# A two-block model on one core: the memory's value projection in the first stage, with uncut float32 operands

## The chip, the cores and the metric

The kernel runs on one core of a Trainium2 chip. The metric is the device time of one execution in microseconds; a time given for a kernel is the median of several runs. Five engines work in one core: TensorE (PE; its weight loads are listed apart as PEld), VectorE (DVE), ScalarE (ACT), GpSimd (POOL) and SyncE (SP), which here issues most DMA transfers.

## The reference, cut to what matters

The model has two blocks over 256 tokens of width 1024: a first block of two layers (a sliding-window attention beside a state-space mixer, then a stick-breaking attention, each followed by a gated feed-forward), and a second block with a feed-forward, a gated mixer, a cross attention to a memory of 256 tokens, and a last feed-forward. The change touches one projection of the cross attention:

```python
def memory_cross_attention(h, m, wq, wk, wv, wo):
    b, s, _ = h.shape
    nm = m.shape[1]
    q = (h @ wq).reshape(b, s, X_HEADS, X_HEAD_DIM)
    k = (m @ wk).reshape(b, nm, X_HEADS, X_HEAD_DIM)
    v = (m @ wv).reshape(b, nm, X_HEADS, X_HEAD_DIM)
    ...
    return o.reshape(b, s, D_MODEL) @ wo
```

Here `m = rmsnorm_2(mem, mem_norm)`. `m @ wv` (256x1024 by 1024x1024) depends on inputs alone, so it can be computed at any time before the cross attention.

## The kernel before

**Weights.** All weight matrices are packed into slabs of 128 partitions by 2048 float32 (1 MB), in the order of use. A slab is loaded over the SP queue into a tile `raw`, of which there are two buffers (`_make`, L270 to L298). Each half of the slab is then cut in two parts in the reduced format fp32r: ScalarE casts it to `whi` (L293), VectorE subtracts to get the rest `wlo` (L295); there are five buffers of half a slab for each. The `raw` buffer is free when both parts of both halves are made. A slab is asked for two slabs ahead of its use (`W_AHEAD`).

**Operands.** The activations are cut in the same way: `_norm` (L443) multiplies the input by the norm's gain, as a high part on ScalarE (L453) and a low part on VectorE (L454), in tiles `a` (four buffers). It also sums the squares: ScalarE squares (L461), GpSimd adds (L463). The inverse root mean square is made in `inv_rms`: column sums on TensorE (L419), a power on GpSimd (L424). It is applied after the product.

**Products.** A product of two cut operands takes three fp32r matmuls (`mm3`, L314 to L322): high by high, high by low, low by high. With operands of one part, `mm3` issues one matmul instead.

**The first stage** (`even`, up to about 130 us). The order in which its parts are written is the string `EVEN`: `p` are the projections of queries, keys and values, `h` the head norms, `i` the four input steps of the state-space mixer, `t` and `s` its tables and scan, `m` and `g` its output products, two digits a step of the window attention, `x` the building of the state matrices on GpSimd (L927 to L929, into tiles `a`), and `N`, `W0` to `W3` the memory's norm and the four slabs of `m @ wv`, each a 256-column part of `mv` (`memory`, L486). The parts of the state matrices are issued on GpSimd after the head norm's last power (`rqk`, L407 and L408), which needs the sums of squares `ssh` (ScalarE L782, VectorE L783). The products of `W` go to an accumulator tile `acc`, of which there are four in PSUM; the state-space inputs hold two of them until the scan has read them. The kernel is written with a framework that orders the instructions of every engine by priority and by a simulated time, so that the order on the engines is not that of the text. Behind the four `W` slabs the plan has two slabs of the output projection, the mixer's gate, and two more output slabs; the first output matmuls are those of `acc<-et,whi`.

In the second block's mix stage, the memory is normed a second time for the keys (`K0` to `K3`), with operands in a pool of that stage.

Of the kernel before, what the change touches and what calls it, by code (L numbers as in the profile page):

```python
# [12 lines left out]
AF = mybir.ActivationFunctionType  # L13
# [3 lines left out]
P = 128  # L17
# [35 lines left out]
def weight_plan():  # L53
# [29 lines left out]
    for f in EVEN.split():  # L83
        if f == "p0":
            tok("even_w_in", 0, 0)
        elif f == "p1":
            feat("even_w_in", 0, 512, 256)
        memory(f)
# [5 lines left out]
    for f in ODD.split():  # L94
        if f[0] == "v":
            tok("odd_w_in", 0, 2048 + int(f[1]) * 512)
        elif f[0] in "qk":
            feat("odd_w_in", 0, (f[0] == "k") * 1024 + int(f[1]) * 256, 256)
        memory(f)
# [4 lines left out]
    for f in MIX.split():  # L104
        if f[0] in "vwxy":
            tok("w_in", 0, 512 + "vwxy".index(f[0]) * 512)
        elif f[0] == "u":
            feat("w_in", 0, int(f[1]) * 256, 256)
        memory(f)
# [13 lines left out]
PR_GAIN, PR_BGLU, PR_ONA, PR_ONB, PR_QN, PR_KN, PR_ARE, PR_AIM, PR_LDT = (  # L123
    0, 80, 84, 88, 92, 93, 94, 110, 126)
# [113 lines left out]
class Kernel:  # L238
# [29 lines left out]
        return self.t(self.sm, shape, tag, dt, bufs)  # L268


    def _make(self, upto, first=None):
        nc = self.nc
        while self.made <= min(upto, len(self.plan) - 1):
            s = self.made
            raw = self.t(self.wp, [P, 2048], "raw", bufs=2)
            if first is None:
                nc.sync.dma_start(raw, self.a["wts"][s])
            else:

                for h, then in enumerate(first):  # L280
                    c = slice(h * 512, (h + 1) * 512)
                    nc.sync.dma_start(self.xt[:, 2 * h:2 * h + 2, :],
                                      self.a["x"][:, c].rearrange("p (b t) -> p b t", b=2))
                    then()
                    nc.sync.dma_start(raw[:, c], self.a["wts"][s][:, c])
            parts = []
            n = 1024 if first is None else 512
            for h in range(2):
                hi = self.t(self.wp, [P, 1024], "whi", F32R, bufs=self.W_BUFS)
                lo = self.t(self.wp, [P, 1024], "wlo", F32R, bufs=self.W_BUFS)  # L290
                for c in range(0, 1024, n):
                    src = raw[:, h * 1024 + c:h * 1024 + c + n]
                    nc.scalar.copy(hi[:, c:c + n], src)  # L293
                    with self.tc.issue_after(self.pin) if self.pin and s > 1 else nullcontext():
                        nc.vector.tensor_tensor(lo[:, c:c + n], src, hi[:, c:c + n].bitcast(F32), ALU.subtract)  # L295
                parts.append((hi, lo))
            self.split[s] = parts
            self.made += 1  # L298
# [144 lines left out]
    def _norm(self, x, gain, tag, make, pool, soon):  # L443
        nc = self.nc
        ops = None
        if make:
            ops = [self.operand(pool, f"m{i}") for i in range(2)]
        ssq = self.t(self.wk, [P, 512], "ssq")
        for pr in range(4):
            for b in (2 * pr, 2 * pr + 1) if make else ():  # L450
                g = self.prm[:, PR_GAIN + gain * 8 + b:PR_GAIN + gain * 8 + b + 1]
                hi, lo = ops[b // 4][0][:, b % 4, :], ops[b // 4][1][:, b % 4, :]
                nc.scalar.activation(hi, x[:, b, :], AF.Copy, scale=g)  # L453
                lo = nc.vector.scalar_tensor_tensor(lo, x[:, b, :], g, hi.bitcast(F32),  # L454
                                                    ALU.mult, ALU.subtract).ins
            q = ssq if pr == 0 else self.t(self.wk, [P, 512], "sq", bufs=2)
            xf = x[:, 2 * pr:2 * pr + 2, :].rearrange("p b t -> p (b t)")
            if gain == 0 and SQE[pr] != "a":
                (nc.gpsimd if SQE[pr] == "g" else nc.vector).tensor_tensor(q, xf, xf, ALU.mult)
            else:  # L460
                nc.scalar.activation(q, xf, AF.Square)  # L461
            if 0 < pr < 3 or pr == 3 and not soon:
                nc.gpsimd.tensor_tensor(ssq, ssq, q, ALU.add)  # L463
        if soon:
            sqs = []
            for x, e in zip((ssq, q), FOLD[gain]):
                if e != "-":
                    (nc.gpsimd if e == "g" else nc.vector).tensor_tensor(x[:, :256], x[:, :256], x[:, 256:], ALU.add)
                sqs += [x[:, c:c + 256] for c in ((0, 256) if e == "-" else (0,))]
        else:  # L470
            nc.gpsimd.tensor_tensor(ssq[:, :256], ssq[:, :256], ssq[:, 256:], ALU.add)
            sqs = [ssq[:, :256]]
        if x is self.xt and make and self.at:
            pin, self.pin = self.pin, lo if PINN else self.pin
            self._make(self.at - 1 + self.W_AHEAD)
            self.pin = pin
        rb, rs = self.inv_rms(sqs, D, 1e-6, tag)
        return ops, rb, rs
# [7 lines left out]
    def memory(self, f, how, pool=None):  # L486
        nc = self.nc
        c = int(f[1:] or 0)
        if f[0] == "N":
            mem = self.t(self.wp, [P, 2048], "raw", bufs=2).rearrange("p (b t) -> p b t", b=8)  # L490
            self.load_feat(mem, self.a["mem"], nc.sync)
            self.mops, self.mrb, self.mrs = self.norm(mem, 8, "mrb", haste=False, pool=pool, soon=how[1])
        elif f[0] == "K":
            if not self.kt:
                self.kt = self.t(self.late, [P, 8, 256], "kt")
            self.gemm_feat(self.mops, "cross_wk", 0, c * 256, 256,
                           self.scaled(self.kt[:, 2 * c:2 * c + 2, :], self.mrb), how[0])
        else:
            if not self.mv:
                self.mv = [self.t(self.values, [P, D], f"mv{t}") for t in range(NT)]  # L500
            w = self.slab("cross_wv", 0, "f", 0, c * 256)
            ps = self.ps(how[0])
            for half in range(2):
                for t in range(NT):
                    for k in range(4 * half, 4 * half + 4):
                        self.mm3(ps[:, t * 256:(t + 1) * 256], self.lhs(self.mops, k, t), w(k * 256, 256),
                                 k == 0 and t == 0, k == 7)
            for t in range(NT):
                nc.scalar.activation(self.mv[t][:, c * 256:(c + 1) * 256], ps[:, t * 256:(t + 1) * 256],
                                     AF.Copy, scale=self.mrs[t])  # L510
# [1055 lines left out]
```

## Time and profile before

| | |
|---|---|
| median of 3 runs | 1231.01 us (1229.61 to 1231.33) |
| the profiled execution | 1231.68 us |
| its span, first to last instruction | 1230.0 us |
| PE busy | 1195.4 us (97%), 7678 matmul records |
| DVE busy | 861.5 us (70%) |
| ACT busy | 681.6 us (55%) |
| POOL busy | 193.4 us (16%) |
| mean granted TensorE clock | 0.987 |

Busy times are of one execution. A busy PE is not a PE at its peak, since matmuls overlap each other: the time between the starts of two matmuls says more than the duration of one.

### The profile page before, as it was taken

How to read it: one execution, taken by the hardware profiler on the slowest of the kernel's cores; microseconds unless marked ns; L12 is line 12 of the kernel's file. 1: busy time of each engine (PE TensorE's matmuls, PEld its weight loads, DVE VectorE, ACT ScalarE, POOL GpSimd, SP SyncE). 2: the span in 40 equal slices, each digit the busy share in tenths (PEclk: the TensorE clock that was granted, in tenths of full speed). 3: DMA queues.
4: the chain of work that ended last, by engine and by line, in shares of the span. 5: the costliest groups of instructions: out<-in, count | busy, mean ns of one | idle time of the engine just before them, and what ended most of it. 6: DMA issues, size and time to landing. Idle time of an engine off the chain costs nothing.

```text
span 1230.0 us, 19039 instructions
## 1 busy us (share of the span) xinstructions
PE 1195.4 (97%) x7678; PEld 1061.6 (86%) x7678; DVE 861.5 (70%) x1196; ACT 681.6 (55%) x1063; POOL 193.4 (16%) x164
## 2 busy tenths in 40 slices
PE   6889999999999999999999999999999999999997
PEld 6767988888898888888888888888879999888886
DVE  8988588776666548777767776666865666777752
ACT  7544565664456757555545655545554545655542
POOL 2295031110010003111002101003201102111000
PEclk9988999999999999999999999999999999999998
DMA  6632345555553234555655555556623534455660
GB/s 241 200 121 87 123 172 202 178 202 202 175 178 137 103 138 171 174 203 179 219 191 184 191 192 184 183 199 203 215 100 104 175 108 162 174 199 178 206 205 35
DMA packets 36777, 208.86 MB, mean 170 GB/s; under 512 B 3921, under 2 KB 9809, under 8 KB 12753
## 3 DMA queue, kind: packets, MB, share of 16 engines
q1 hardware_dynamic: 35824, 205.48, 48.4%
q0 software_dynamic: 576, 1.64, 0.5%
q8 instruction: 60, 0.98, 0.3%
q10 hardware_dynamic: 288, 0.52, 0.1%
q14 instruction: 29, 0.23, 0.1%
HBM read 205.57 MB, written 2.06 MB: 169 GB/s over the span
## 4 chain that ended last, share of the span: by engine, by line
PE 74%; DMA 8%; DVE 7%; ACT 5%; POOL 3%; issue 3%; SPq 0%; DVEq 0%; ACTq 0%; POOLq 0%
PE acc L367 23%; PE acc L366 12%; PE mm L367 10%; DMA raw<-in_wts 6%; PE mm L366 5%; PE acc L321 3%; PE acc L320 3%; PE acc L322 3%; PE mm L320 3%; PE mm L321 3%; PE mm L322 3%; DVE wlo L295 3%; ACT whi L293 3%; POOL a L927 1%; DMA raw<-in_mem 1%
## 5 line engine op out<-in xcount | busy, mean ns | idle before, releaser
L295 DVE TENSOR_TENSOR wlo<-raw,whi 128x1024 fp32r<-128x1024 f32 (+1 forms) x378 | 470.5, 1248 | 235.1 <-ACT whi L293 233.1
L293 ACT CAST whi<-raw 128x1024 fp32r<-128x1024 f32 (+1 forms) x378 | 393.1, 1046 | 279.5 <-DMA raw<-in_wts 117.1
L367 PE MATMUL mm<-a,whi 128*128 128x512 f32 x704 | 247.0, 392 | 0.0
L367 PE MATMUL acc<-h,whi 128*128 128x512 f32 x704 | 246.8, 396 | 0.0
L367 PE MATMUL acc<-a,whi 128*128 128x512 f32 x704 | 245.8, 391 | 0.0
L366 PE MATMUL acc<-h,wlo 128*128 128x256 f32 x704 | 196.9, 281 | 0.4 <-ACT h L549 0.4
L366 PE MATMUL mm<-a,wlo 128*128 128x256 f32 x704 | 196.5, 281 | 0.0
L366 PE MATMUL acc<-a,wlo 128*128 128x256 f32 x704 | 196.2, 280 | 0.0
L367 PEld LDWEIGHTS acc<-h,whi 128*128 128x128 f32 x704 | 131.8, 188 | 31.0
L367 PEld LDWEIGHTS mm<-a,whi 128*128 128x128 f32 x704 | 131.5, 187 | 28.5
L367 PEld LDWEIGHTS acc<-a,whi 128*128 128x128 f32 x704 | 130.9, 187 | 28.1
L366 PEld LDWEIGHTS acc<-a,wlo 128*128 128x128 f32 x704 | 133.0, 189 | 0.9
L366 PEld LDWEIGHTS acc<-h,wlo 128*128 128x128 f32 x704 | 132.9, 189 | 1.1 <-ACT h L549 0.7
L366 PEld LDWEIGHTS mm<-a,wlo 128*128 128x128 f32 x704 | 132.6, 189 | 0.2
L546 POOL TENSOR_TENSOR sg<-sg,rb 128x512 f32<-128x512 f32 x44 | 58.3, 1326 | 391.7 <-ACT sg L545 391.7
L463 POOL TENSOR_TENSOR ssq<-ssq,sq 128x512 f32<-128x512 f32 x26 | 40.2, 1544 | 420.6 <-ACT sq L461 250.1
L320 PE MATMUL mm<-a,whi 128*128 128x256 f32 x224 | 65.3, 293 | 7.3 <-ACT whi L293 6.4
L321 PE MATMUL acc<-a,whi 128*128 128x256 f32 x240 | 67.6, 285 | 0.0
L322 PE MATMUL acc<-a,wlo 128*128 128x256 f32 x240 | 67.4, 285 | 0.0
L322 PE MATMUL mm<-a,wlo 128*128 128x256 f32 x224 | 64.8, 290 | 1.4 <-DVE wlo L295 1.3
L320 PE MATMUL acc<-a,whi 128*128 128x256 f32 x240 | 65.9, 285 | 0.0
L321 PE MATMUL mm<-a,whi 128*128 128x256 f32 x224 | 64.5, 289 | 0.0
(369 smaller groups left out, 1912.3 us busy)
## 6 DMA issues: line engine op xcount, KB each, us to landing
raw<-in_wts SPq DMA_DIRECT2D x187, 1024.0 KB, 4.9
raw<-in_mem SPq DMA_DIRECT2D x4, 512.0 KB, 5.7
eb<-lag SPq DMA_DIRECT2D x4, 512.0 KB, 5.2
x<-in_x SPq DMA_DIRECT2D x4, 256.0 KB, 5.1
raw<-in_wts SPq DMA_DIRECT2D x4, 256.0 KB, 5.3
sprm<-in_prm SPq DMA_DIRECT2D x1, 512.0 KB, 9.4
ud<-s SPq DMA_DIRECT2D x1, 512.0 KB, 3.2
uu<-ud SPq DMA_DIRECT2D x8, 64.0 KB, 5.9
```

Of the source, the lines that this page charges most:

```text
L293: nc.scalar.copy(hi[:, c:c + n], src)
L295: nc.vector.tensor_tensor(lo[:, c:c + n], src, hi[:, c:c + n].bitcast(F32), ALU.subtract)
L320: mm(out, a[0], b[0], start=start, stop=False, skip_group_check=True)
L321: mm(out, a[0], b[1], start=False, stop=False, skip_group_check=True)
L322: mm(out, a[1], b[0], start=False, stop=stop, skip_group_check=True)
L366: mm(out[:, 0, :], w[1], x[:, 0], start=first, stop=False, skip_group_check=True)
L367: mm(out, w[0], x, start=False, stop=last, skip_group_check=True)
L463: nc.gpsimd.tensor_tensor(ssq, ssq, q, ALU.add)
L546: nc.gpsimd.tensor_tensor(sg, sg, rb2, ALU.mult)
L927: eng.tensor_tensor(out, f(pr), h(xr), ALU.mult)
```

## The change

The four slabs of `cross_wv` are no longer cut: the slab's halves in `raw` are handed to the product as one-part operands of float32. The memory's operand in the first stage is one float32 tile of 8 blocks (memory times gain, on ScalarE), again of one part, so `mm3` issues one float32 matmul where it issued three fp32r ones. The second norm of the memory, in the mix stage, keeps its cut operands.

```diff
+    @staticmethod
+    def whole(key):
+
+        return key[0] == "cross_wv"
+
     def _make(self, upto, first=None):
...
+            if self.whole(self.plan[s]):
+                self.split[s] = [(raw[:, :1024],), (raw[:, 1024:],)]
+                self.made += 1
+                continue
             parts = []
...
     def _norm(self, x, gain, tag, make, pool, soon):
         nc = self.nc
         ops = None
-        if make:
+        if make == "whole":
+            y = self.t(self.ap4, [P, 8, 256], "a", bufs=self.A_BUFS)
+            ops, make = [(y[:, :4],), (y[:, 4:],)], False
+            for b in range(8):
+                g = self.prm[:, PR_GAIN + gain * 8 + b:PR_GAIN + gain * 8 + b + 1]
+                nc.scalar.activation(y[:, b, :], x[:, b, :], AF.Copy, scale=g)
+        elif make:
             ops = [self.operand(pool, f"m{i}") for i in range(2)]
...
-            self.mops, self.mrb, self.mrs = self.norm(mem, 8, "mrb", haste=False, pool=pool, soon=how[1])
+            self.mops, self.mrb, self.mrs = self.norm(mem, 8, "mrb", pool is not None or "whole", haste=False,
+                                                      pool=pool, soon=how[1])
```

## Rows read from the trace of the kernel before

**Rows 1.** Stretches: length, busy time (instructions) of five engines, clock, DMA share, GB/s.
```profile
44.00:62.00 18.00, 15.89 (x149) 14.79 (x147) 16.90 (x24) 11.42 (x24) 7.36 (x6) 0.91 0.52 185
78.00:98.00 20.00, 14.86 (x136) 10.43 (x136) 14.99 (x24) 7.56 (x26) 19.22 (x17) 0.79 0.22 66
105.00:130.00 25.00, 24.55 (x246) 21.71 (x245) 18.95 (x29) 13.48 (x29) 4.36 (x4) 1.00 0.40 130
130.00:1230.00 1100.00, 1086.18 (x6771) 967.83 (x6771) 754.62 (x1023) 609.42 (x914) 130.22 (x107) 1.00 0.49 171
```

**Rows 2.** Instructions of TensorE in order of time: start, duration, line, operation, out<-in, count.
```profile
104.94 0.38 PE L320 MATMUL acc<-whi,a 128*128 128x256 f32 x1
...
110.67 0.28 PE L322 MATMUL acc<-whi,a 128*128 128x256 f32 x1
...
118.63 0.28 PE L322 MATMUL acc<-whi,a 128*128 128x256 f32 x1
...
119.33 0.32 PE L1088 MATMUL acc<-a,sprm 128*64 128x128 f32 x1
...
129.29 0.60 PE L320 MATMUL acc<-et,whi 128*128 128x256 f32 x3
```

**Rows 3.** GpSimd in order of time; in brackets idle time before and its releaser.
```profile
59.40 1.09 POOL L424 TENSOR_TENSOR rs<-rs,nhalf 128x2 f32<-128x2 f32 x1 [6.10 <-DVE rs L423]
61.61 0.78 POOL L407 TENSOR_SCALAR rqk<-ssh 128x10 f32<-128x10 f32 x1 [1.11 <-DVE ssh L783]
...
70.91 2.09 POOL L927 TENSOR_TENSOR a<-sp_pr,sp_nci 128x512 f32<-128x512 f32 x1
...
76.07 2.08 POOL L927 TENSOR_TENSOR a<-sp_pr,sprm 128x512 f32<-128x512 f32 x1
...
79.17 1.09 POOL L927 TENSOR_TENSOR a<-sp_pr,sprm 128x512 f32<-128x512 f32 x1
...
93.78 1.26 POOL L929 TENSOR_TENSOR eb<-eb,otmpg 128x512 f32<-128x512 f32 x1
```

**Rows 4.** VectorE in order of time.
```profile
60.10 1.23 DVE L295 TENSOR_TENSOR wlo<-raw,whi 128x1024 fp32r<-128x1024 f32 x1 [0.17 <-ACT whi L293]
61.24 0.28 DVE L783 TENSOR_REDUCE ssh<-sq 128x2 f32<-128x128 f32 x1
...
69.90 4.18 DVE L295 TENSOR_TENSOR wlo<-raw,whi 128x1024 fp32r<-128x1024 f32 x2
...
101.19 0.68 DVE L1037 TENSOR_TENSOR s<-acc,s2c 128x512 f32<-128x512 f32 x1
...
114.81 1.35 DVE L1051 TENSOR_TENSOR bdc<-eb,s 64x496 f32<-64x496 f32 x2
```

**Rows 5.** ScalarE in order of time.
```profile
53.09 0.47 ACT L769 ACTIVATE qkv<-mm,rs 128x256 f32<-128x256 f32 x1
59.01 1.06 ACT L293 CAST whi<-raw 128x1024 fp32r<-128x1024 f32 x1 [5.44 <-DMA raw<-in_wts]
59.97 0.83 ACT L782 ACTIVATE sq<-qkv 128x128 f32<-128x128 f32 x2
```

**Rows 6.** Cross scores on TensorE: durations (min/median/max ns) of line L1415; part in order of time.
```profile
L1415 PE MATMUL mm<-kt,qt x32: 377/379/382, 987.5 to 1004.9; 128*128 128x256 f32 x32
...
988.46 2.75 PE L1415 MATMUL mm<-kt,qt 128*128 128x256 f32 x12
```

**Rows 7.** Groups of VectorE, 25 to 130 us: count | busy us, mean ns | idle before.
```profile
L295 DVE TENSOR_TENSOR wlo<-raw,whi 128x1024 fp32r<-128x1024 f32 x18 | 24.1, 1350 | 2.8 <-ACT whi L293 2.8
```

**Rows 8.** Loads issued by SP, in order of time.
```profile
39.98 0.85 SPq L658 DMA_DIRECT2D raw<-in_mem  x2
43.31 15.10 SPq L277 DMA_DIRECT2D raw<-in_wts  x3
...
66.44 8.00 SPq L277 DMA_DIRECT2D raw<-in_wts  x2
```

**Rows 9.** DMA issues of the page: count, KB each, us to landing.
```profile
raw<-in_wts SPq DMA_DIRECT2D x187, 1024.0 KB, 4.9
```

## The prediction

> **What bounds the kernel now.** I read the stretches first, then the chain of waits, then each engine's instructions in order of time along it. From 130 us to the end TensorE's matmuls are busy 1086.2 of 1100 us [rows 1]: nothing of the change lies there, and a time won or lost before 130 us is handed on whole. Before it TensorE has holes: 14.9 of 20 us from 78 to 98, at a granted clock of 0.79 [rows 1]. From 105 on it is full again, 24.55 of 25 us [rows 1]. So the question is what sets the moment at which the first output projection starts, 129.29 us [rows 2].
>
> The chain of waits, read backwards from there, leads through TensorE to GpSimd's `eb` of the last state step, which ends at 95.04, and GpSimd comes there through an almost unbroken run of outer products that starts behind the head norm's two `rqk` pairs; the first starts at 61.61, released by VectorE's reduction `ssh` [rows 3]. That reduction (61.24) stands behind a `wlo` at 60.10 [rows 4], and its squares (59.97) stand on ScalarE behind the cast `whi` at 59.01, which had idled 5.44 us for a weight load [rows 5]. By order of the loads that slab is W2, the third of the four touched here. VectorE is busy 16.9 of 18 us from 44 to 62 [rows 1]. So a slab that nobody needs until the cross stage holds up the head norm, and with it GpSimd.
>
> **The change, part by part.** All sums stand against the profiled execution, 1231.68 us (a span of 1230.0 and 1.7 around it); the median shown, 1231.01, is 0.7 lower.
>
> *TensorE.* Removed: 4 slabs x 16 products x 3 reduced matmuls = 192. W2's 48 start between 104.94 and 110.67, so 5.73/47 = 0.122 us each [rows 2]: 5.85 a slab. Added: 64 uncut matmuls of 128x256. The cross scores are this very form: 16 matmuls in the program, 32 records, 12 of them in 2.75 us, the last lasting 0.38, so 2.37/11 = 0.215 us a record [rows 6], two records a matmul, 0.43 us. 16 x 0.43 = 6.9 us a slab, +1.05; over four slabs +4.2. W0 and W1 run earlier, while the chain is on VectorE and GpSimd: cost 0, and +2.1 if that cover is gone. W2 and W3 run in the full stretch after 104.94: **+2.1**. At the lower of the clock's levels all of these double; the stretch after 105 was granted 1.00 [rows 1].
>
> The rule that speaks against the change agrees in kind and differs in size. The Trainium skill (FP8 and Floating Point Precision, TensorE Precision Notes) says that true float32 takes four passes through the array. With the reduced matmul's step for a pass that is 4 x 0.122 = 0.49 us a product, +2.0 a slab, so +4.0 instead of +2.1 here; the two records of the row are shorter than that, and I go by the row.
>
> *VectorE and ScalarE.* Eight `wlo` halves go, 1.35 us each on average [rows 7], eight `whi` halves of 1.06 [rows 5], and the memory's eight `a` subtractions. The eight scaled copies on ScalarE stay in number, as uncut ones. The part on the path: W2's cast no longer stands before the squares. At least its wait of 5.44 goes; at most all from the end of the second `qkv` copy (53.09 + 0.47 = 53.56) to the end of that cast (60.07), 6.5 us [rows 5]. At the other end 0, or worse, is the second rival below. I take **-5.4**, the wait itself: the memory's own work on ScalarE now comes later (next part) and will eat some of the rest.
>
> *GpSimd.* Its outer-product multiply takes 2.09 us at 70.91, while VectorE works on W3's two `wlo` (69.90 to 74.08, 2.09 each instead of a typical 1.2), and 1.09 us at 79.17 without one [rows 3, 4]. Three such long ones start between 70.91 and 76.07 (2.09, 2.09, 2.08); the first two lie beside W3's. Those `wlo` go: 2 x 1.0 = **-2.0**, on the chain. Bounds: 0, if other two-input work of VectorE moves in beside them; -3.0, if the third goes too (its `wlo` is the first output slab's, which is only moved).
>
> *The raw buffers.* There are two, and an uncut slab holds its own until its matmuls have read it. W0 thus holds one while the memory wants one: the memory's load, at 39.98 before, now waits for the next projection slab's split, after which the following weight load went at 43.31 [rows 8], so +3.3 us on the memory. W1's load waits for the memory as before; W2's and W3's for W0's and W1's matmuls; and the first two output slabs, loaded at 66.44 and 74.11 [rows 8], now for W2's and W3's. The last of W3's matmuls ends about 119 [rows 2]. A load lands after 4.9 us [rows 9]; two casts and a subtraction make the second output slab ready some 8.2 us after W3's end. It is wanted one slab (5.8 us) after the first output matmul, and that follows W3's end by 10: wanted after 16, there after 8. Cost 0; were the 8 us of cover gone, each microsecond more would cost one. The same moves bring one more split into the stretch from 105 to 130, where VectorE has 6 us free: 0, at most 1.2.
>
> *The operand.* One tile instead of two, in the same slots: nothing waits for a slot there, 0.
>
> Sum: -5.4 - 2.0 + 2.1 = -5.3, so 1226.4 for an execution like the profiled one and **1225.7** against the median. With 0 to -6.5, 0 to -3.0 and +2.1 its own range is 1222 to 1229.
>
> **Rivals.**
>
> *W2 goes into the hole.* Uncut, W2 is ready when its load lands. If it is put behind W1 before 98 us, the stretch after 105 loses a slab. Then VectorE's scan limits it: the last state copy ends at 116.16 [rows 4], the state products start at 119.33 [rows 2]: -3.2, and the +2.1 is hidden. Total -5.4 - 2.0 - 3.2 = -10.6: 1220.4. For: TensorE's hole. Against: W2's product needs one of four accumulator banks, and started soon after the scan's readings of the two state banks (101.19 to 101.87) [rows 2, 4].
>
> *Slower: the memory norm stays ahead on GpSimd.* The memory's power (59.40) stands before the `rqk` pairs in GpSimd's queue [rows 3]. If it keeps that place while the memory's load is 3.3 us later, it ends at about 63.8 and `rqk` starts there or later: +2.2 on the chain at the least, +3.3 if all behind it slides. With +2.1 to +4.2 from TensorE and the -2.0 given back by later collisions, that is +4.3 to +7.5. I take +4.3: 1235.3. It decides as soon as the memory's power stands before the first `rqk`. For: it did before. Against: the squares of the heads are then ready some 5 us before it, and the queue's order follows readiness.
>
> *A wash.* The head norm comes forward by only the 2.1 that W2 and W3 cost, because the memory's twelve copies and squares on ScalarE push in front of the head norm's, and the collisions on GpSimd only change partners: 1231.
>
> *It doesn't do what it says.* Were an uncut product run as one reduced pass, four slabs would cost a third of 23.4 us, but the scores' two records a product [rows 6] speak against it.
>
> **How the numbers follow.** Forecast 0.42; W2 in the hole 0.20; slower 0.20; wash 0.12; an order laid out anew for other reasons 0.06, half of it slower. What this measurement can tell from no change is 0.2%, 2.5 us. Faster: 0.42 x 0.95 + 0.20 + 0.02 = 0.62; within: 0.12 + 0.02 + 0.01 = 0.15; slower: 0.23. The range goes from W2 in the hole with all bounds on its side, 1217, to the slower case, 1236; about 0.2 stays outside.
>
> **What would show it.** Right: `rqk` starts at 55 to 57; no idle of 5 us on ScalarE before the head squares; the outer products about 1.1 us throughout 62 to 75; `eb` ends near 87.6; a W slab's 32 records take 6.9 us; the first output matmul stands at about 124. Wrong: the first `rqk` at or after 61; W2's records before 98 (first rival); ScalarE idling for the second output slab's load, or TensorE idling before it; any change after 130 us that is not a mere shift.

## The result, and the profile after

The changed kernel takes **1253.41 us** (median of 4 runs, 1249.46 to 1258.57), the kernel before 1231.17 (4 runs): a ratio of 1.0169 [1.0147, 1.019]. It is slower by 22 us; I had said 1225.7. Its profiled execution took 1254.56 us, a span of 1252.8. Lines up to the products stand 9 further down in its text, those of the first stage 16.

The same stretches as in [rows 1], of the changed kernel; columns as there:

```profile
44.00:62.00 18.00, 18.00 (x144) 16.20 (x141) 8.87 (x14) 9.48 (x22) 10.55 (x9) 1.00 0.49 165
78.00:98.00 20.00, 19.32 (x109) 12.94 (x108) 10.63 (x20) 6.78 (x22) 11.56 (x9) 0.50 0.07 19
105.00:130.00 25.00, 23.20 (x115) 18.47 (x112) 16.49 (x22) 6.34 (x18) 9.70 (x7) 0.79 0.27 87
130.00:1230.00 1100.00, 1087.76 (x6818) 967.54 (x6817) 759.38 (x1027) 614.02 (x923) 127.83 (x105) 1.00 0.50 173
```

VectorE is relieved from 44 to 62 (8.87 us busy, 16.9 before), as meant. From 78 to 98 TensorE is busy almost throughout, at a granted clock of 0.50, its lower level, and from 105 to 130 the clock is 0.79 where it was 1.00.

GpSimd, against [rows 3]:

```profile
54.48 0.21 POOL L416 TENSOR_SCALAR rqk<-ssh 128x10 f32<-128x10 f32 x1 [2.13 <-DVE ssh L799]
...
57.75 0.69 POOL L433 TENSOR_TENSOR rs<-rs,nhalf 128x2 f32<-128x2 f32 x1 [1.01 <-DVE rs L432]
...
62.61 1.10 POOL L943 TENSOR_TENSOR a<-sp_pr,sprm 128x512 f32<-128x512 f32 x1
...
71.68 1.10 POOL L943 TENSOR_TENSOR a<-sp_pr,sp_nci 128x512 f32<-128x512 f32 x1
...
85.89 1.61 POOL L943 TENSOR_TENSOR eb<-sp_pr,sp_bbi 128x512 f32<-128x512 f32 x1 [9.37 <-PE tr L1022]
...
94.03 1.59 POOL L945 TENSOR_TENSOR eb<-eb,otmpg 128x512 f32<-128x512 f32 x1
```

The head norm's first power starts 7.1 us earlier (54.48), and the outer products into `a` take 1.10 us each. The first of them, which stands behind both pairs of `rqk`, starts 5.6 us earlier (62.61) than in the kernel before:

```profile
68.19 1.11 POOL L927 TENSOR_TENSOR a<-sp_pr,sprm 128x512 f32<-128x512 f32 x1
```

Then GpSimd idles 9.37 us for TensorE, and its last `eb` ends at 95.62, about where it ended before (95.04).

TensorE, against [rows 2], with the two waits that matter, the end of the state-space inputs (`acc<-uu,et`) and the last four attention scores (L607):

```profile
73.01 1.06 PE L1094 MATMUL acc<-eb,uu 128*32 128x128 f32 x10 [3.58 <-DMA eb<-lag]
...
104.59 1.07 PE L1015 MATMUL acc<-uu,et 128*64 128x32 f32 x16
...
108.47 7.18 PE L327 MATMUL acc<-raw,a 128*128 128x256 f32 x32
...
119.44 1.22 PE L607 MATMUL mm<-ktw,s 64*128 64x256 f32 x2
...
123.73 8.15 PE L327 MATMUL acc<-raw,a 128*128 128x256 f32 x32
...
133.41 0.70 PE L607 MATMUL mm<-ktw,s 64*128 64x256 f32 x2
...
143.78 1.08 PE L410 MATMUL tr<-ident,prob 128*128 128x128 f32 x4 [4.48 <-DVE prob L628]
...
149.61 0.61 PE L329 MATMUL acc<-et,whi 128*128 128x256 f32 x3
```

The same places in the kernel before, where the wait for the first `eb<-lag` is 2.53 us long and another one is for GpSimd's last `eb`:

```profile
80.79 0.64 PE L1078 MATMUL acc<-eb,uu 128*32 128x128 f32 x16 [2.53 <-DMA eb<-lag]
...
95.09 0.66 PE L401 MATMUL tr<-ident,eb 128*128 128x128 f32 x4 [2.50 <-POOL eb L929]
...
99.47 1.07 PE L999 MATMUL acc<-uu,et 128*64 128x32 f32 x16
...
111.11 1.13 PE L591 MATMUL mm<-ktw,s 64*128 64x256 f32 x4
```

SP's loads, against [rows 8], and ScalarE's part of the end:

```profile
111.53 0.32 SPq L1031 DMA_DIRECT2D lag<-lsb  x1
119.35 0.37 SPq L1088 DMA_DIRECT2D eb<-lag  x1
119.77 20.20 SPq L282 DMA_DIRECT2D raw<-in_wts  x4
```

```profile
136.18 1.99 ACT L302 CAST whi<-raw 128x1024 fp32r<-128x1024 f32 x2 [2.07 <-DMA raw<-in_wts]
...
139.11 1.28 ACT L1107 ACT_TABLE_LOAD   x1
...
141.02 1.28 ACT L624 ACT_TABLE_LOAD   x1
142.31 0.20 ACT L624 ACTIVATE es<-es 128x2 f32<-128x2 f32 x1
```

W2's product ends at 115.65 and frees its `raw`, but the first output slab's load goes at 119.77: on SP it stands behind the last state matrix's load `eb<-lag`. In the kernel before all four last scores run at 111.1, ahead of W3; here two of them (133.41) run behind W3. What follows them, the exponential `es` (142.31), queues on ScalarE behind the late slab's casts (136.18, after 2.07 us of waiting for the load) and two table loads; TensorE idles 4.48 us for it.

Four moments of the profiled executions give the sum:

| us | before | after | lost since the row above |
|---|---|---|---|
| last state-space input matmul ends | 100.54 | 105.66 | 5.1 |
| first output matmul starts | 129.29 | 149.61 | 15.2 |
| first feed-forward matmul starts | 158.24 | 179.49 | 0.9 |
| end of the span | 1230.0 | 1252.8 | 1.6 |

So two questions: why the gain of 6 to 7 us on GpSimd is a loss of 5 at the state-space inputs (the **middle**), and why the way from there to the first output matmul, the **tail**, takes 44.0 us in place of 28.75.

### The profile page after: what moved, and what is told of

Read it like the earlier page. It is cut to its first block, busy times and chain, and to the rows that moved or that the text cites. A ratio compares the mean times of both kernels' runs of the same rounds, so it can differ in the third digit from the quotient of the medians.

```text
span 1252.8 us, 18876 instructions
## 1 busy us (share of the span) xinstructions
PE 1215.4 (97%) x7614; PEld 1071.5 (86%) x7614; DVE 843.0 (67%) x1180; ACT 673.4 (54%) x1057; POOL 187.7 (15%) x164
## 4 chain that ended last, share of the span: by engine, by line
PE 52%; DMA 7%; DVE 5%; ACT 4%; issue 2%; POOL 0%; DVEq 0%; ACTq 0%; SPq 0%; POOLq 0%
PE acc L376 16%; PE acc L375 8%; PE mm L376 6%; DMA raw<-in_wts 6%; PE mm L375 3%; PE mm L329 2%; DVE wlo L304 2%; ACT whi L302 2%; PE mm L330 2%; PE mm L331 2%; PE acc L330 2%; PE acc L329 2%; PE acc L331 2%; PE mm L1463 1%; PE mm L1431 1%
## 5 line engine op out<-in xcount | busy, mean ns | idle before, releaser
L304 DVE TENSOR_TENSOR wlo<-raw,whi 128x1024 fp32r<-128x1024 f32 (+1 forms) x370 | 459.4, 1245 | 240.3 <-ACT whi L302 238.7
L302 ACT CAST whi<-raw 128x1024 fp32r<-128x1024 f32 (+1 forms) x370 | 383.9, 1043 | 284.7 <-DMA raw<-in_wts 121.1
```

## The experiments

All eighteen in one table; the ratio is to the kernel before on the same chip. "Clock" is the granted clock from 60 to 100 us; the next columns are the end of the state-space inputs, the length of the tail, and the time from the first feed-forward matmul to the end. These four columns are of one execution of each run, which can lie up to 5 us beside the median (e3: 1238.9 for a median of 1243.6; e9: 1243.1 for 1238.0).

| run | us | ratio | clock | inputs end | tail | rest |
|---|---|---|---|---|---|---|
| before | 1231.2 | 1 | 0.87 | 100.5 | 28.8 | 1071.7 |
| changed kernel | 1253.4 | 1.0169 [1.0147, 1.0190] | 0.64 | 105.7 | 44.0 | 1073.3 |
| e1 slabs copied out | 1237.6 | 1.0042 [1.0025, 1.0058] | 0.66 | 101.3 | 30.5 | 1073.9 |
| e2 before, `raw` held | 1241.3 | 1.0070 [1.0049, 1.0091] | 0.70 | 105.4 | 33.8 | 1070.3 |
| e3 before, one product | 1243.6 | 1.0088 [1.0071, 1.0104] | 0.73 | 105.9 | 30.4 | 1071.2 |
| e4 W2 early | 1239.9 | 1.0059 [1.0035, 1.0082] | 0.93 | 107.0 | 28.8 | 1076.5 |
| e5 before, four products | 1244.2 | 1.0091 [1.0070, 1.0111] | 0.81 | 106.0 | 33.7 | 1073.2 |
| e6 e3 + ten matmuls | 1243.3 | 1.0085 [1.0064, 1.0105] | 0.91 | 101.8 | 32.5 | 1078.4 |
| e7 e1 + ten matmuls | 1237.6 | 1.0039 [1.0023, 1.0056] | 1.00 | 93.2 | 31.5 | 1078.6 |
| e8 e1, W1 later | 1249.4 | 1.0137 [1.0114, 1.0160] | 0.66 | 97.0 | 38.3 | 1073.9 |
| e9 W0, W1 uncut | 1238.0 | 1.0045 [1.0031, 1.0060] | 0.66 | 109.8 | 28.9 | 1073.9 |
| e10 W2, W3 uncut | 1235.9 | 1.0023 [1.0011, 1.0035] | 0.88 | 99.8 | 32.9 | 1072.6 |
| e11 changed + ten matmuls | 1241.5 | 1.0071 [1.0046, 1.0096] | 0.88 | 97.9 | 32.6 | 1079.1 |
| e12 before again | 1234.8 | one run | 0.76 | 101.0 | 28.9 | 1074.3 |
| f1 changed, SP order | 1250.4 | 1.0151 [1.0132, 1.0169] | 0.66 | 106.0 | 40.3 | 1071.0 |
| f2 changed + 8 columns | 1242.4 | 1.0085 [1.0061, 1.0108] | 0.68 | 100.8 | 37.5 | 1072.8 |
| f3 changed, order mended | 1242.3 | 1.0080 [1.0061, 1.0099] | 0.64 | 105.0 | 35.2 | 1073.4 |
| f4 before + 8 columns | 1232.1 | 0.9995 [0.9983, 1.0007] | 0.85 | 99.4 | 31.7 | 1073.1 |
| g1 e7 again | 1236.5 | one run | 0.96 | 95.3 | 30.7 | 1079.3 |
| g2 e1 again | 1230.4 | one run | 0.83 | 96.8 | 30.6 | 1071.9 |

### The buffers, the products, an earlier W2

e1, the changed kernel with each uncut slab copied out of `raw`:

```diff
+                h0 = self.t(self.wp, [P, 1024], "whi", F32, bufs=self.W_BUFS)
+                h1 = self.t(self.wp, [P, 1024], "wlo", F32, bufs=self.W_BUFS)
+                nc.scalar.copy(h0, raw[:, :1024])
+                nc.vector.tensor_copy(h1, raw[:, 1024:])
+                self.split[s] = [(h0,), (h1,)]
...
```

> The changed kernel, but each of the four slabs is copied uncut out of its raw buffer (one half by ScalarE, one by VectorE, no subtraction), so the raw buffer is free before the matmuls. Theory 'held raw buffers' (W2 and W3 hold both raw buffers until 115.6 and 131.9 us, so the output slabs load from 119.8 us on and their casts stand before the attention's exponentials): most of the loss goes, 1229 to 1236 us. Theory 'clock' (W0 and W1 are done before 68 us, nothing dense is left for TensorE until 108 us, and the clock stands at its lower level): stays at 1246 to 1254 us. Theory 'matmul time' (uncut products cost 1.1 us a slab): 1246 or more.

e2, the kernel before, in which one column of `raw` is read again behind the slab's product:

```diff
...
+            nc.vector.tensor_tensor(self.small([P, 1], "hold"), self.raws[self.at - 1][:, :1],
+                                    self.mv[1][:, c * 256:c * 256 + 1], ALU.add)
```

> The kernel before, with cut slabs and three reduced matmuls, but the raw buffer of each of the four slabs is read once more (one column) after the slab's product is copied out, so that it is held as long as in the changed kernel. Theory 'held raw buffers': 1243 to 1255 us with nothing else changed. Theories 'clock' and 'matmul time': 1230 to 1235 us.

e3, the kernel before with one uncut matmul of the two high parts (the low parts are left out of the product, here and in e6, e9 and e10):

```diff
+                        self.mm3(ps[:, t * 256:(t + 1) * 256], [self.lhs(self.mops, k, t)[0].bitcast(F32)],
+                                 [w(k * 256, 256)[0].bitcast(F32)],
...
```

> The kernel before, splits, loads and releases as they are, but the four slabs' products are one uncut float32 matmul of the high parts where there were three reduced ones (the low parts are left out of the product). Theory 'matmul time': the uncut matmuls alone cost 2 to 5 us, 1233 to 1236 us, and if they also lower the clock by themselves 1240 or more. Theories 'held raw buffers' and 'clock' as an effect of the moved order: 1230 to 1234 us.

e4, the changed kernel with `W2` ahead of `m0` in `EVEN`:

> The changed kernel, with W2 written six steps earlier in the order of the first stage (before the state mixer's first output products). Theory 'clock': W2 gives TensorE dense work between 68 and 100 us, the granted clock there rises from 0.50 to 0.8 or more, and the time falls to 1235 to 1242 us. Theory 'held raw buffers': one raw buffer is free some 40 us earlier, the first output slab loads before 100 us, the second still late: 1238 to 1246 us. If W2 stays behind the scan for want of an accumulator bank, both expect no change, 1248 to 1256 us.

e5, the kernel before with a fourth reduced product, low by low:

> The kernel before with the cut operands kept, and a fourth reduced product, low part by low part, added to the three of each W slab; nothing uncut. By the matmul records of before (0.12 us each, 16 more a slab) a slab then keeps TensorE some 1.9 us longer, about as the uncut products did in the run with uncut products of the high parts alone, which took 1243.6. Theory 'the uncut form itself' (it lowers the granted clock or costs something beside its records): this run stays at 1233 to 1236, with two short spells at the lower clock as before. Theory 'longer slabs shift the phase' (any longer W0 and W1 put the hole ahead of the first memory slab where the clock falls for long): 1240 to 1244 with a spell of 17 us or more at the lower clock between 60 and 105 us.

Copying the slabs out gives back 15.8 us, most of it in the tail (30.5 for 44.0); at 1237.6 the time is 1.6 above what 'held raw buffers' allowed. Holding `raw` costs 8 us (e2; 1241.3 where I expected 1243 to 1255), and this is not the price of the buffers alone: in its trace the order on every engine differs from that of the kernel before.

e5 costs as much as e3 without anything uncut, so nothing here shows a price of the uncut form beyond its time. But both cost 10 to 11 us where the longer products of W2 and W3 explain 2 and 4; their buffers and loads are as before, while their traces show another order on every engine too. What the rest of those 10 us is was not settled.

e4 lies in the ranges of two theories (1239.9). It fills the hole with W2, the clock rises to 0.93, and it gains nothing in the middle: TensorE then idles 7.6 us for `es`, which stands on VectorE behind two `wlo`. Its gain is the tail: the two output slabs are loaded at 76.7 and 94.7 and the tail is 28.8 us, that of the kernel before.

### Ten matmuls in the hole

Ten plain float32 matmuls of 128x256 at the place where TensorE waits for the first `eb<-lag` (in the expectations, the first memory slab's load). In the trace of e6 they are 20 records in 4.48 us, twice the 2.2 that its expectation names:

```diff
...
+            for _ in range(10 if q == 0 else 0):
+                nc.tensor.matmul(yb[0][:, :256], self.ident, dense, start=True, stop=True, skip_group_check=True)
```

> The kernel with uncut products of the high parts alone (the low parts are left out of the product), and ten plain float32 matmuls of 128x256 added behind the first head scores, whose result is overwritten: about 2.2 us of TensorE work at the place where it waits for the first memory slab's load. Theory 'clock': the hole is filled, the granted clock between 60 and 100 us comes back from 0.73 to 0.85 or more, the state inputs end 4 to 5 us earlier (101 in place of 105.9) and the time is 1236 to 1239 in place of 1243.6. Theory 'matmul time': the fillers are only more work: 1243 to 1246.

> The changed kernel with each W slab copied uncut out of the raw buffer (1237.6 without fillers) and the same ten filler matmuls added (their result is overwritten). Theory 'clock': between 60 and 100 us the granted clock rises from 0.66 to 0.85 or more, the state inputs end some 4 to 7 us earlier (95 to 97 in place of 101.3), and the time falls to 1230 to 1234, as fast as before or faster. Theory 'TensorE isn't what the head waits for there' (the chain through GpSimd and VectorE sets the state inputs): 1236 to 1240, whatever the clock.

e8, e1 with `W1` behind `m0 m1 00` in `EVEN`:

> The changed kernel with each W slab copied uncut out of the raw buffer, and its slabs issued in another order: W1 behind the first two memory slabs' loads and the first outer block, W2 later too, so that real work stands in the place of the fillers. Theory 'clock': W1's products fill the hole, the granted clock between 60 and 100 us is 0.8 or more and the time is 1230 to 1235. Theory 'TensorE isn't what the head waits for': 1237 or more, since W1 now stands in front of the memory's products.

> The changed kernel and ten plain float32 matmuls of 128x256 added at the place where TensorE waits for the first memory slab's load; their result is overwritten. Theory 'clock': the long spell at the lower clock (71 to 108 us) goes, the state inputs end 5 to 9 us earlier than in the changed kernel (97 to 101 in place of 105.7), and, as the tail behind W3 stays, the time is 1243 to 1249 in place of 1253.4. Theory 'the head gains and the rest gives it back', as the copied slabs with fillers did in the median (1237.64 beside 1237.60): 1250 to 1255 with the state inputs early. Theory 'clock plays no part': the state inputs stay at 105 and the time at 1252 to 1256.

> The kernel before, once more, unchanged. It shows how much of what the profiles differ in is by the execution: if its spells at the lower clock before 130 us are again four short ones of 3.4 to 6.8 us (20.4 us in all) and the state inputs end within 1 us of 100.5, then the long spells of the variants are theirs; if it shows a spell of 17 us or more and still takes 1231 to 1235, the spells are no explanation of the times.

The clock rose and the inputs ended 4, 8 and 8 us earlier (e6, e7, e11), but the medians of e6 and e7 stayed where those of e3 and e1 were: the clock and the inputs came as the first theory said, the times as the second. In the profiled executions the way from the first feed-forward matmul to the end is 7.2 and 4.7 us longer than in e3 and e1 (below).

e8 failed in its aim: W1 ran at 98 to 105, behind the inputs, and the tail carried three slabs. e11 gave back 12 us, 1.5 more than the most that its theories allowed; in its profile 8 are from the middle and 11 from the tail, where no matmul had been added, less 6 lost behind. The framework had laid out another order there.

e12 speaks against the clock as the whole answer: the kernel before shows a long spell at the lower clock too (81 to 105 us, row below) at 1234.8 us, which by its expectation means that the spells by themselves don't explain the times. Its inputs end at 101.0, half a microsecond later than in the first execution. TensorE, which was busy for 21.39 of these 24 us in the first execution and idled 2.50 for `eb`, is busy for all of them here, so part of what the lower clock costs went into time in which it had idled.

```profile
81.00:105.00 24.00, 24.00 (x158) 16.97 (x155) 17.96 (x29) 6.50 (x23) 20.68 (x17) 0.50 0.09 26
```

### One half of the slabs at a time

```diff
+            if self.plan[s][0] == "cross_wv" and self.plan[s][4] in (0, 256):
+                self.split[s] = [(raw[:, :1024],), (raw[:, 1024:],)]
...
```

e10 has `(512, 768)` there.

> Only W0 and W1 are handed over uncut, W2 and W3 are cut as before (for the two uncut slabs the memory's low part is left out of the product; its cut operand is still made). Theory 'held raw buffers, in the tail': the two late slabs free their buffers early again, so the output slabs are loaded before 90 us, and from the end of the state inputs to the first output matmul it takes 28 to 31 us as in the kernel before (28.75), not 44; the time is 1231 to 1241, by whether the clock falls for long between 60 and 105 us. Theory 'early slabs cost as much as late ones' (W0 and W1 hold the memory's load and the next slabs back, and that is carried on): 1243 or more.

> Only W2 and W3 are handed over uncut, W0 and W1 are cut as before (the memory's low part is left out of W2's and W3's product). Theory 'held raw buffers, in the tail': W2 and W3 hold both buffers, the output slabs are loaded only behind their matmuls, after 115 us, and the way from the end of the state inputs to the first output matmul is 36 us or more in place of 28.75; the time is 1240 to 1252. Theory 'early slabs': W0 and W1 run as before, so the time is 1231 to 1236.

e9 came as the first theory said, with the output slabs loaded at 71.3 and 83.9. e10 refutes it in size: both late slabs hold both buffers, the output slabs are loaded at 111.7 and 120.1, and the tail is 32.9 us, not 36 or more; the time, 1235.9, is not 1240 or more either. The two halves cost 5.1 and 3.0 us; the changed kernel costs 22. Held buffers alone are not the cause.

The loads of all runs agree with that. Where the second output slab is asked for before 95 us (the kernel before, e1, e3 to e9, e12, f4, g1, g2) the tail is 28.8 to 33.7 us, but for e8 with its three slabs (38.3). Where it is asked for after 117 us (e2, e10, e11, f1 to f3, the changed kernel) it is 32.6 to 44.0. So a late load can go with a tail only 4 to 5 us longer than before (e2, e10, e11); the changed kernel's 15 need more than that.

### The order that the framework lays out

f1, the changed kernel with one edge of order on SP (every other engine's order is unchanged):

```diff
...
+            with self.tc.issue_after(self.first_out) if q == 3 else nullcontext():
                 nc.sync.dma_start(m, win)
```

> The changed kernel, in which SP issues the first output slab's load ahead of the last state matrix's load; the order of every other engine is the same. Theory 'order on SP': the load goes at about 115.7, when W2's product has ended, in place of 119.8, its casts come 4 us earlier, and the time is 1248 to 1251 in place of 1253.4. Theory 'order on TensorE' (W3 ahead of the last attention scores sets the end, whatever the loads): 1252 to 1255. Theory 'clock': 1252 to 1255 too.

f2, one of the ten matmuls, 8 columns wide:

> The changed kernel and one matmul of 8 columns, under 0.1 us of work, whose result is overwritten. It doesn't fill the hole, but the planned order comes out nearly as in the run with ten added matmuls (on SP the same; 42 of some 1300 TensorE instructions elsewhere). Theory 'order': 1240 to 1244, as with ten (1241.5). Theory 'clock in the hole': 1250 to 1256, as without any.

f3, f1 with `W3` behind `13` in `EVEN`, and held behind the last scores:

```diff
...
+                        with self.tc.issue_after(self.score) if c == 3 and k + t == 0 else nullcontext():
```

> The changed kernel with two orders mended by hand: the first output slab's load ahead of the last state matrix's on SP, and W3 behind the last attention scores on TensorE. Nothing is done about the hole or the clock. Theory 'order': the way from the end of the state inputs to the first output matmul falls from 44 to 28 to 34 us, and the time is 1239 to 1245. Theory 'raw buffers by themselves' (the second output slab's load waits for W3 all the same, and W3 now stands last): 40 us or more and 1249 or more. Theory 'clock': the state inputs stay at 105 or later, and at most the tail's lower clock (two spells of 6.8 us) is given back, 1247 or more.

> The kernel before and the same matmul of 8 columns: the planned order stays but for 2 instructions on TensorE and 2 on VectorE. Both theories: 1231 to 1236, as without it; if it moves by more than 3 us, small changes of order alone are worth as much as the effects that are told apart here.

f1: SP's queue, the load now at 115.09 and the state matrix's behind it; the tail is 3.7 us shorter, the median 3.0, as the first theory said. The intervals of the two ratios overlap, so the time by itself would not show it; the rows do.

```profile
115.09 0.33 SPq L282 DMA_DIRECT2D raw<-in_wts  x1
119.68 0.37 SPq L1091 DMA_DIRECT2D eb<-lag  x1
```

f2: two records that last 0.29 us together, which fill nothing (the clock is 0.50 from 74.5 to 101), and 11 us come back: in its profile 4.8 in the middle (the inputs end at 100.8) and 6.5 in the tail. TensorE's rows show the order: all four last scores ahead of W3.

```profile
111.33 1.13 PE L607 MATMUL mm<-ktw,s 64*128 64x256 f32 x4
...
118.72 8.79 PE L327 MATMUL acc<-raw,a 128*128 128x256 f32 x32
...
138.29 0.60 PE L329 MATMUL acc<-et,whi 128*128 128x256 f32 x3
```

f3: the middle is as bad as in the changed kernel (inputs 105.0, clock 0.64), the last scores stand ahead of W3, and the tail falls from 44.0 to 35.2 us, the time to 1242.3. The length missed what I expected (28 to 34) by 1 us, the time is inside it. Some instructions on VectorE and ScalarE change their places along with the two orders.

```profile
123.00 0.70 PE L610 MATMUL mm<-ktw,s 64*128 64x256 f32 x2
...
129.21 4.58 PE L329 MATMUL acc<-raw,a 128*128 128x256 f32 x20
...
140.16 0.62 PE L331 MATMUL acc<-et,whi 128*128 128x256 f32 x3
```

The control f4 doesn't move the time.

### The same two programs again

> The copied slabs with ten added matmuls, once more. Theory 'the head gains, the feed-forwards give it back': the first feed-forward's first matmul stands again at 153 to 156 us (158.2 before) and the way from there to the end takes 1076 us or more (1071.7 before). Theory 'one execution': the first feed-forward starts at 158 or later, or the rest takes 1070 to 1074.

> The copied slabs without added matmuls, once more. Theory 'the clock holds up the head': again a spell of 20 us or more at the lower clock from about 71 us on, the state inputs at 100 to 103 us and the rest at 1072 to 1075. Theory 'one execution': a short spell and the state inputs at 93 to 96.

g2 is e1's program, order and all, in another execution. Neither expectation came as it was put: the lower clock lasts 14 us, and the inputs end at 96.8. Two stretches, first of e1, then of g2:

```profile
71.00:85.00 14.00, 11.93 (x99) 9.18 (x102) 4.23 (x11) 4.89 (x15) 11.99 (x12) 0.51 0.25 75
85.00:99.00 14.00, 13.33 (x54) 8.77 (x47) 7.95 (x15) 4.37 (x15) 11.73 (x9) 0.52 0.02 5
```

```profile
71.00:85.00 14.00, 12.13 (x102) 9.36 (x105) 4.42 (x11) 5.09 (x15) 11.98 (x12) 0.52 0.24 72
85.00:99.00 14.00, 12.43 (x116) 8.62 (x109) 11.51 (x23) 5.57 (x20) 13.37 (x11) 0.99 0.02 6
```

Both fall to the lower clock at 71, behind a wait of 3.1 us for `eb<-lag`. In g2 the clock is back at 85, in e1 only at 99; GpSimd's `eb` ends at 88.3 in e1 and at 88.1 in g2, yet the inputs end 4.5 us apart (101.3 and 96.8). Here TensorE, not GpSimd, sets the pace, and the longer spell at the lower clock costs these 4.5 us. The time of g2, 1230.4, is below all nine of e1 (1234.4 to 1242.8).

g1 repeats e7: the first feed-forward starts at 155.3 (158.2 before), and the rest takes 1079.3. From 1100 to 1170 us its TensorE waits; the kernel before shows no such wait there, and the order in that stretch is the same in both (in all, times, longest):

```profile
PE mm L379 <- DVE wlo L308: 2.1, 2, 1.2
PE acc L379 <- ACT h L569: 2.0, 1, 2.0
```

All four runs with the ten matmuls lose 6.7 to 7.6 us behind the first feed-forward matmul, the others at most 4.8 (e4); 2.6 of it the kernel before loses as well in its second execution (e12). Which condition brings the stream of slabs into this step was not settled.

## Why the prediction was wrong, point by point

- **The head norm and GpSimd** (-5.4): right. The first power came at 54.48 (I said 55 to 57), ScalarE's 5 us of idling is gone, and the first outer product stands 5.6 us earlier. **The collisions** (-2.0): right in kind, 1.10 us a product; the third long one went too, so it is the bound of 3.0 that came.
- **What is late next** was not asked. I let the gain run through to `eb` at 87.6. Where TensorE keeps up that far, it does: 88.3 in e1, 86.7 in e11. But with W0 and W1 done by 67.7 instead of 73.4, TensorE has nothing to do while it waits for the first `eb<-lag`; the clock falls at 71 and stays down until 108, and GpSimd waits 9.37 us for TensorE. That the clock alone does this is not shown: f2, at 0.50 from 74.5 to 101 like the changed kernel, ends the inputs at 100.8, and e4, at 0.93, ends them at 107.0. The row of before that should have warned me was in my first group: 0.79 from 78 to 98 [rows 1].
- **W2 and W3** (+2.1): the size is right, W2 takes 7.18 us for the 6.9 that I worked out (W3, partly at the lower clock, 8.15). The four passes of the Trainium skill (FP8 and Floating Point Precision, TensorE Precision Notes) would have made it 7.8, an estimate by the reduced step of 0.122. The trace shows two records of 0.22 us, so four passes could stand if a pass takes 0.11 us, an estimate too; the step that I gave a pass was too long.
- **The raw buffers** (0) are the step that failed: the tail that hangs on them took 15.2 us more. I put the first output matmul 10 us behind W3's end, as in [rows 2], and gave the second slab 8 us of cover; both took the old order for granted. The first slab's load went 4 us after its buffer was free, behind a DMA that I had not listed in SP's queue; W3 was put ahead of two of the last scores; W3's end to the first output matmul became 17.7 us. Shown: the SP order 3.7 us of tail (f1), both orders 9 us of tail and some 11 of the time (f3); f2 gets the same 11 by another order. What remains between those runs and e1, 1242 to 1238, some 5 us, I take for the buffers' own price; e1's order is another one again, so this is a difference and not a measurement of it.
- **The framework's order.** I gave 0.06 to an order laid out anew. The code orders by a simulated time, and this change altered durations, buffers and operands of four slabs; f2 shows that 8 columns are enough to move 11 us.
- **The rival that came out slower** had the wrong mechanism: the memory's power (57.75) did go behind the first `rqk`. **W2 in the hole** did not happen; forced (e4), it made no gain in the middle.
- Of the marks that I had named as wrong, ScalarE idled for the second output slab's load (2.07 us), and TensorE idled before the first output matmul (4.48 us).
- **The range.** My own bounds don't give 1222 to 1229: against the median, -6.5, -3.0 and +2.1 make 1223.6, and 0, 0 and +2.1 make 1233.1. Neither of them lets the buffers cost anything, and neither reaches 1253.

Beside the kernel before on each chip, the changed kernel costs 22.2 us, f2 and f3 cost 9.7 and 9.6, e1 costs 4.5. By these differences order accounts for some 12 us and held buffers for some 5, and 4 to 5 are left. In these I see the longer W2 and W3, and a gain of the head that the clock ate, as e1 and g2 show it for that program. That the clock cost the changed kernel itself its 5 us in the middle is argued, not shown: e11, which filled the hole, changed the order as well, and f2 got them back without filling it.

## What to carry to other kernels

Where a framework orders by simulated time, a change of duration or of buffer lifetime is a change of order: read where the neighbouring loads and fillers may land, and run the change with a negligible instruction added before calling its effect its own. An operand used where it was loaded pins the load buffer until its last reader; a copy out cost less here than the pin. And a filler that is moved forward leaves a hole where it was: look whether the clock falls there, and whether TensorE then sets the pace, as in e1 beside g2, or has idle time to give, as in e12.

## What was not expected of the hardware

TensorE stayed at the lower of its two levels while it was busy: 33.57 of 35 us from 73 to 108 in the changed kernel, granted 0.50, after 3.58 us of waiting for a DMA.

```profile
69.00:73.00 4.00, 0.43 (x3) 0.12 (x1) 0.29 (x1) 0.69 (x1) 4.00 (x5) 0.77 0.78 259
73.00:108.00 35.00, 33.57 (x209) 23.95 (x210) 17.59 (x35) 9.82 (x31) 19.35 (x16) 0.50 0.14 41
```

The Trainium skill (TensorE: Matmul & The Clock Gate, HAM oscillation — how this bites in real kernels) tells of waits for DMAs behind which the next matmuls start at the lower clock; the fall here agrees. What this case adds is how long the clock stays down while TensorE is busy. The work in this stretch is small matmuls and transposes, and the clock of one and the same program, e1's, came back after 14 us in one execution (g2) and after 27 in another (e1).
